# Moving the fourth weight strip's split behind the further blocks of an expert, and side-by-side high and low parts for short second and third blocks

## The chip, the cores and the metric

The kernel runs on one core of a Trainium2 chip. The metric is the time of one execution on the device in microseconds (us); of several runs the median counts.

## The reference

One decoder layer on 2048 tokens of 1024 channels, all in fp32. A first half (projections, a state-space branch, a convolution branch, gates, an output projection, a LayerNorm) gives `h`. The second half, which matters here, is a mixture of 32 SwiGLU experts of inner width 256. Every token picks two experts, so there are 4096 assignments:

```
hid = silu(xb @ w_gate[e]) * (xb @ w_up[e])      # xb: rows of h that chose expert e
y   = hid @ w_down[e]                            # added to the token's row with its weight
out = LayerNorm(ALPHA * h + sum of the two y)
```

The reference, run on its own inputs, sends these numbers of rows to experts 0 to 31:

```
121  75 114  74 129  25 158 106 205 200 227  36 276 286 255 177
 50  58 174 160  11 119 273  99  42  54 130 211  60  77  19  95
```

In blocks of 128 rows that is 49 blocks. Seventeen of them are a second or third block of their expert. Nine of those hold at most 64 rows: the second blocks of experts 4, 6, 15, 18, 19 and 26 (1, 30, 49, 46, 32 and 2 rows) and the third blocks of 12, 13 and 22 (20, 30 and 17 rows).

## The kernel before, in words

The program is one list of instructions for each engine, in an order written by hand; an instruction waits only where its data or its buffer is not ready. fp32 precision comes from splitting every operand into a high part (fp32r) and a low part, and from three matmuls for each product: high by high, high by low, low by high.

**Routing.** In the output projection, for each pair of token tiles, `route1` picks the experts, `rank` (on PE) numbers the rows within an expert and `route2` (lines 1189 to 1210) turns the number into a slot of a table `td` in DRAM and scatters token and weight there, four POOL DMAs a pair. The last pair's `route2` runs after the last output projection. Then ACT reads the table back (`lists`, line 1380), POOL gathers the rows of expert 0 from `hd`, and PE starts on the experts.

**The expert loop** (lines 1520 to 1552) goes over e = 0 to 31, with two sets of buffers, j = e % 2. Weights come in six strips for each expert: strips 0 to 3 are gate and up weights (128x1024 each, in `eraw`, split into `egu`), strips 4 and 5 are the down weights (`erd`, split into `edn`). `high` (line 1242) is ACT's copy to the high part, `low` (line 1247) DVE's subtraction that leaves the low part; `step` does both. While expert e is computed, the strips of expert e+1 are split, and the weights of e+3 are loaded by SP into the buffer that the split has emptied: `load` in four DMAs of 512 KB, the first two for strips 0 and 1, the last two for strips 2 and 3, and `load2` with one of 1 MB.

One round for expert e, in program order:

1. POOL gathers the rows of the block after (e+1, 0) and, if e has more than 128 (256) rows, those of the block after (e, 1) (and after (e, 2)).
2. `step` of strips 0, 1, 2 of e+1, then `high` of strip 3.
3. `block` (line 1471): `gateup`, 24 matmuls `pg<-egu,bhl` (eight channel strips times three products) into one PSUM bank, then `act`: ACT's Silu of the gate half, DVE's product with the up half (`hid`).
4. `low` of strip 3, and the four `load` DMAs of e+3.
5. `turn`: PE turns the rows of the next block (8 transposes `pt`), ACT copies the high part and DVE subtracts for the low part of `bhl`.
6. `down` of the expert before (12 matmuls `pd`).
7. `further(e, 1)` (line 1476), a branch at line 1486 that PE, ACT, DVE and POOL each take for themselves. With more than 128 rows it turns `hid` (two transposes `ph`), emits the finished rows (ACT copies PSUM to `yy` in two halves; between them `splith`, which is `hh` on ACT and `hl` on DVE; then POOL's scatter with addition into `acc`), and does block, turn and down for the second block, and inside it the same for a third. With fewer rows it only turns `hid`.
8. The end-of-expert `emit` with `splith`, then `high` and `low` of strips 4 and 5 of e+1, and `load2` of e+3.

`bhl` is a tile of 128 partitions, 8 strips, 2 parts (high, low) and 128 columns (rows of the block). `gateup` takes one part of one strip, 128x128, as the stationary operand and 512 columns of weights as the moving one.

`select` (line 1383) works out on DVE, from the table and the counts, which rows are gathered after which block (`NX`) and which rows and weights each emit uses (`LL`, `LQ`).

Of the kernel before, what the change touches and what calls it, by code (L numbers as in the profile page):

```python
# [10 lines left out]
F32 = mybir.dt.float32  # L11
# [15 lines left out]
NE = 32  # L27
# [58 lines left out]
def layer(ctx, tc, a, out, dbg=None):  # L86
# [976 lines left out]
    def small(name, shape, dt=F32):  # L1063
        return dp.tile([128] + list(shape), dt, name=name, bufs=2)
# [124 lines left out]
    def route2(p, pk):  # L1189
        ef, oh, ob, sd = RT_.pop(p)  # L1190
        for t in range(2):
            V.tensor_tensor(ohs, ohs, ob[:, t, :], op=OP.add)
        V.tensor_tensor(oh, oh, pk.unsqueeze(2).to_broadcast([128, 2, 2, 32]), op=OP.mult)

        rk, sl = small("r_rk", [2, 2]), rc_.tile([128, 2, 2], I32, name="r_sl", bufs=2)
        V.tensor_reduce(rk, oh, axis=AX.X, op=OP.add)
        dv = oh[:, :, :, 0]
        V.tensor_scalar(dv, rk, 1.0 / 128.0, -0.498, op0=OP.mult, op1=OP.add)
        V.scalar_tensor_tensor(rk, rk, 32.0, ef, op0=OP.mult, op1=OP.add)
        V.tensor_scalar(dv, dv, MAGIC, None, op0=OP.add)  # L1200
        V.tensor_scalar(dv, dv, MAGIC, -65535.0, op0=OP.subtract, op1=OP.mult)
        V.scalar_tensor_tensor(sl, rk, 16.0, dv, op0=OP.mult, op1=OP.add)
        for t in range(2):
            for k in range(2):
                G.memset(spacer, 0.0)
                d = G.indirect_dma_start(out=td, out_offset=bass.IndirectOffsetOnAxis(ap=sl[:, t, k:k + 1], axis=0),  # L1206
                                         in_=sd[:, t, k, :], in_offset=None)
                for o in SC:
                    tc.declare_no_dep(d.ins, o.ins, reason="other rows of the table")
                SC.append(d)  # L1210
# [146 lines left out]
    HH = ep.tile([128, 2, 128], F32R, name="hh")  # L1357
    HL = ep.tile([128, 2, 128], F32R, name="hl")
    HID = ep.tile([128, FF], F32, name="hid")
    TAB = ep.tile([128, NE, JB, 2], I32, name="tab")  # L1360
    MK = ep.tile([128, NE, JB], F32, name="mk")
    OH = ep.tile([128, NE, JB], F32, name="ohb")
# [14 lines left out]
    V.tensor_tensor(OH[:, :, 0:JB - 1], MK[:, :, 0:JB - 1], MK[:, :, 1:JB], op=OP.subtract)  # L1377
    V.tensor_copy(OH[:, :, JB - 1:JB], MK[:, :, JB - 1:JB])

    def lists(e, n):  # L1380
        A.dma_start(TAB[:, e:e + n].rearrange("p e b c -> p e (b c)"), dap(td, 32 * e, [[1024, 128], [32, n], [1, 2 * JB]]))

    def select():


        V.tensor_copy(TF[:, 0:NE], TAB[:, :, :, 0])
        V.memset(TF[:, NE:NE + 1], float(1 << 20))
        first = TF[:, 1:NE + 1, 0:1]
        t = LP[:, :, 0:JB - 1, 0]
        V.tensor_tensor(t, TF[:, 0:NE, 1:JB], first.to_broadcast([128, NE, JB - 1]), op=OP.subtract)  # L1390
        V.tensor_tensor(t, t, MK[:, :, 1:JB], op=OP.mult)
        V.tensor_tensor(NX[:, :, 0:JB - 1], t, first.to_broadcast([128, NE, JB - 1]), op=OP.add)
        V.tensor_copy(NX[:, :, JB - 1:JB], first)
        V.tensor_tensor(LP[:, :, :, 0], TF[:, 0:NE], OH, op=OP.mult)
        V.tensor_tensor(LP[:, :, :, 1], TAB[:, :, :, 1].bitcast(F32), OH, op=OP.mult)
        lf = TF[:, 0:NE, 0:2]
        V.tensor_reduce(lf, LP.rearrange("p e b c -> p e c b"), axis=AX.X, op=OP.add)
        V.tensor_copy(LL[:, :, 0], lf[:, :, 0])
        V.tensor_copy(LL[:, :, 1].bitcast(F32), lf[:, :, 1])
        V.tensor_copy(LP[:, :, 0:JB - 1, 0], TAB[:, :, 0:JB - 1, 0])  # L1400
        V.tensor_tensor(LP[:, :, 0:JB - 1, 0], LP[:, :, 0:JB - 1, 0], OH[:, :, 1:JB], op=OP.mult)
        V.tensor_tensor(LP[:, :, 0:JB - 1, 1], TAB[:, :, 0:JB - 1, 1].bitcast(F32), OH[:, :, 1:JB], op=OP.mult)
        V.tensor_tensor(LP[:, 1:NE, JB - 1], lf[:, 0:NE - 1], OH[:, 1:NE, 0:1].to_broadcast([128, NE - 1, 2]), op=OP.mult)
        V.memset(LP[:, 0:1, JB - 1], 0.0)
        V.tensor_reduce(lf, LP.rearrange("p e b c -> p e c b"), axis=AX.X, op=OP.add)
        V.tensor_copy(LQ[:, :, 0], lf[:, :, 0])
        V.tensor_copy(LQ[:, :, 1].bitcast(F32), lf[:, :, 1])
# [30 lines left out]
    def act(i):  # L1438
        A.activation(HID, PG[i][:, 0:FF], AF.Silu)
        V.tensor_tensor(HID, HID, PG[i][:, FF:2 * FF], op=OP.mult)  # L1440

    def turnh():
        for k in range(2):
            PE.transpose(PH[:, k, :], HID[:, 128 * k:128 * k + 128], ident)

# [24 lines left out]

    def block(e, b, i, gu):

        gateup(i, gu)
        act(i)

    def further(e, b):

# [29 lines left out]
    load2(2, 0)  # L1507
    lists(0, 2)
    lists(2, NE - 2)
    gather(X1, TAB[:, 0, 0, 0:1])  # L1510
    high(1, 2, 3, 4, 5)
    low(1, *range(6))
# [7 lines left out]
    for e in range(NE):  # L1520
# [10 lines left out]
                    gather(X2, NX[:, e, 2:3])  # L1531
        if more:
            step(1 - j, 0, 1, 2)
            high(1 - j, 3)
        block(e, 0, j, GU[j])
        if more:
            low(1 - j, 3)
            if e + 3 < NE:
                load(e + 3, 1 - j)
        turn(XN[j])  # L1540
        if e:
            down(1 - j)
        further(e, 1)
        if e:
            emit(LQ[:, e, 0:1], LQ[:, e, 1:2], splith)
        else:
            splith()
# [167 lines left out]
```

## Time and profile before

| | |
|---|---|
| median of 3 runs | 1854.08 us (1853.65 to 1859.51) |
| the profiled execution | 1854.43 us, its span 1852.7 us |
| PE, PEld, DVE busy | 92%, 74%, 71% of the span |
| ACT, POOL busy | 37%, 17% |
| the expert stage, first to last gate-and-up block | 1281.3 to 1771.9 us of the span |
| mean granted TensorE clock | 0.968 |

PE is TensorE's matmuls, PEld its loads of stationary operands, which overlap them; DVE is VectorE, ACT ScalarE, POOL GpSimd, SP the queue that issues most loads. Busy shares are means over stages with different limits, so the stretches below are read one by one. A matmul's row lasts longer than its distance to the next (they are pipelined), so PE's pace is read from the starts. In a timeline a square bracket gives the engine's idle time before the row and what ended it; DVEq L1486 is DVE's own passing of the branch of `further`. Line 66 is the helper through which all PE and DVE instructions go.

### The profile page before, as it was taken

The page shows a single profiled execution, that of the slowest core. Times are in us where ns is not written, and L with a number is a line of the kernel's source. Part 1 is how long each engine was busy: PE and PEld are TensorE (multiplying, and loading weights), DVE is VectorE, ACT ScalarE, POOL GpSimd, SP SyncE. Part 2 cuts the span into 40 slices and gives each one's busy share as a digit, 9 for nine tenths or more (in the row PEclk, how much of TensorE's full clock was granted, in tenths as well). Part 3 has the DMA queues.
Part 4 walks back from the last instruction along what each step waited for, and adds up shares of the span by engine and source line. Part 5 has one row for each costly group of instructions (what it writes and reads, how often), then busy time and mean ns, then how long its engine had stood idle before and what let it go on. Part 6 is the DMA issues. An engine that isn't in the chain of part 4 may idle for free. (4 is left out here: it accounts for less than half of the span.)

```text
span 1852.7 us, 23925 instructions
## 1 busy us (share of the span) xinstructions
PE 1703.9 (92%) x8368; PEld 1371.0 (74%) x8369; DVE 1317.4 (71%) x2429; ACT 692.4 (37%) x1069; POOL 312.6 (17%) x319
## 2 busy tenths in 40 slices
PE   8999999999999999999999999973999999999930
PEld 7888877777777778777888888862777787777730
DVE  5798787777876874766576778885675556657648
ACT  5111221222222222633321122324675556666744
POOL 2000001101110101000000012212343233333315
PEclk9999999999999999999999999986999999999975
DMA  6321432432342336333463423546988878789755
GB/s 215 95 92 46 119 78 71 145 98 77 100 149 70 101 99 222 109 122 114 172 191 119 148 92 115 182 164 197 304 266 256 253 211 253 230 261 327 223 176 231
DMA packets 214027, 300.81 MB, mean 162 GB/s; under 512 B 29391, under 2 KB 159521, under 8 KB 211313
## 3 DMA queue, kind: packets, MB, share of 16 engines
q1 hardware_dynamic: 166496, 213.32, 35.0%
q0 software_dynamic: 23152, 56.06, 11.6%
q10 hardware_dynamic: 24224, 29.47, 4.8%
q8 instruction: 86, 1.41, 0.3%
q14 instruction: 69, 0.56, 0.1%
HBM read 224.77 MB, written 92.31 MB: 171 GB/s over the span
## 5 line engine op out<-in xcount | busy, mean ns | idle before, releaser
L66 PE MATMUL mm<-xh,whi 128*128 128x512 f32 x896 | 360.8, 403 | 0.0
L66 PE MATMUL mm<-xl,whi 128*128 128x512 f32 x896 | 353.6, 395 | 0.0
L66 PE MATMUL mm<-xh,wlo 128*128 128x512 f32 x896 | 352.1, 393 | 0.0
L66 PE MATMUL pg<-egu,bhl 128*128 128x512 f32 x1176 | 287.4, 399 | 25.1 <-DVEq L1486 20.7
L66 DVE SCALAR_TENSOR_TENSOR cvw<-cvw,cw 128x1024 f32<-128x1024 f32 x240 | 292.1, 1280 | 0.0
L66 PEld LDWEIGHTS pg<-egu,bhl 128*128 128x128 f32 x1176 | 217.9, 189 | 78.1 <-issue 14.2
L66 PEld LDWEIGHTS mm<-xh,whi 128*128 128x128 f32 x896 | 168.3, 188 | 47.9 <-ACT y L712 5.8
L66 PEld LDWEIGHTS mm<-xh,wlo 128*128 128x128 f32 x896 | 168.2, 188 | 41.6
L66 PEld LDWEIGHTS mm<-xl,whi 128*128 128x128 f32 x896 | 168.6, 188 | 36.5 <-DVE xl L66 0.3
L66 PE MATMUL mm<-yt,whi 128*128 128x512 f32 x512 | 163.7, 401 | 2.0 <-ACT yt L858 1.5
L66 PE MATMUL mm<-wo,mh 128*128 128x512 f32 x512 | 162.5, 398 | 0.0
L66 DVE TENSOR_TENSOR egu<-eraw,egu 128x1024 fp32r<-128x1024 f32 x128 | 150.7, 1218 | 6.0 <-ACT egu L1245 5.9
L731 ACT ACTIVATE gt<-mm,cols 128x512 f32<-128x512 f32 x64 | 44.0, 688 | 265.4 <-PE mm L66 254.4
L66 PE MATMUL pd<-edn,hh 128*128 128x512 f32 x392 | 126.7, 404 | 1.0 <-ACT hh L1447 1.0
L1245 ACT ACTIVATE egu<-eraw 128x1024 fp32r<-128x1024 f32 x128 | 124.9, 1056 | 3.3 <-DMA td<-r_sd,r_sl 3.1
L66 PEld LDWEIGHTS mm<-yt,whi 128*128 128x128 f32 x512 | 96.6, 190 | 25.8 <-ACT yt L858 1.5
L66 PEld LDWEIGHTS mm<-wo,mh 128*128 128x128 f32 x512 | 94.2, 188 | 21.5 <-issue 1.2
L66 PE MATMUL mm<-yt,wlo 128*128 128x512 f32 x256 | 101.5, 396 | 0.0
L66 PE MATMUL mm<-wo,ml 128*128 128x512 f32 x256 | 101.0, 394 | 0.0
L66 DVE TENSOR_TENSOR edn<-erd,edn 128x1024 fp32r<-128x1024 f32 x64 | 75.7, 1225 | 33.0 <-ACT edn L1245 33.0
L1206 POOL DMA_INDIRECT td<-r_sd,r_sl x32 | 38.2, 1194 | 310.3 <-DVE r_sl L66 300.9
L1465 POOL DMA_INDIRECT acc<-yy,lq x31 | 49.2, 1589 | 244.8 <-ACT yy L1462 244.8
(300 smaller groups left out, 2561.3 us busy)
## 6 DMA issues: line engine op xcount, KB each, us to landing
eraw<-in_w_gate_dram SPq DMA_DIRECT2D x64, 512.0 KB
eraw<-in_w_up_dram SPq DMA_DIRECT2D x64, 512.0 KB
erd<-in_w_down_dram SPq DMA_DIRECT2D x32, 1024.0 KB
gd<-gt ACTq DMA_DIRECT2D x64, 256.0 KB
gl<-gd SPq DMA_DIRECT2D x64, 256.0 KB
wraw<-in_w_in_dram SPq DMA_DIRECT2D x28, 512.0 KB
xt<-in_x_dram SPq DMA_DIRECT2D x16, 512.0 KB
rg<-in_x_dram SPq DMA_DIRECT2D x8, 1024.0 KB
```

What stands on the lines that cost most here:

```text
L66: return f(*args, **kw)
L731: A.activation(gt, p, AF.Sigmoid, bias=cols[:, BI + 12 + m:BI + 13 + m])
L1206: d = G.indirect_dma_start(out=td, out_offset=bass.IndirectOffsetOnAxis(ap=sl[:, t, k:k + 1], axis=0), in_=sd[:, t, k, :], in_offset=None)
L1245: A.activation(h, src, AF.Copy)
L1465: G.indirect_dma_start(out=acc, out_offset=bass.IndirectOffsetOnAxis(ap=idx, axis=0), in_=y, in_offset=None, bounds_check=S - 1, oob_is_er ...
```

## The change

Four things are done.

- **Slots.** `route2` numbers the rows of a block so that the first 64 go to the even partitions (0, 2, 4, ...) and the next 64 to the odd ones. That takes eight small DVE operations in place of five.
- **Short blocks.** A second or third block of at most 64 rows goes through `gateup_small` and `act_small`. Its stationary operand is every second column of both parts of a strip, 64 high columns and 64 low ones side by side (`BE`), against the high and then the low part of the weights: 16 matmuls in place of 24. PSUM rows 0 to 63 then hold the products of the high parts, rows 64 to 127 those of the low parts; ACT copies the lower half to SBUF, DVE adds the upper one, and Silu and product follow on 64 rows. The choice is a branch inside the branch of `further`, on the same four engines. First blocks are untouched.
- **Lists.** A second copy of the table, `TB2`, read by one more DMA on ACT's queue, holds the rows of even slots close together; `select` gets eight more DVE operations and the set-up before it eight (`SM`, `NM`: which experts end in a short block), so that the emit of a short block writes the right rows. ACT zeroes `HID` once.
- **The fourth strip.** `high` of strip 3 leaves its place ahead of the first block, `low` of strip 3 and the `load` of e+3 leave theirs behind it. All three stand after `further(e, 1)` and before the end-of-expert emit.

```
 route2:
         dv = oh[:, :, :, 0:2]
         V.tensor_scalar(dv[:, :, :, 0], rk, 1.0 / 128.0, -0.498, op0=OP.mult, op1=OP.add)
+        V.tensor_scalar(dv[:, :, :, 1], rk, 1.0 / 64.0, -0.498, op0=OP.mult, op1=OP.add)
-        V.scalar_tensor_tensor(rk, rk, 32.0, ef, op0=OP.mult, op1=OP.add)
+        V.scalar_tensor_tensor(rk, rk, 64.0, ef, op0=OP.mult, op1=OP.add)
         V.tensor_scalar(dv, dv, MAGIC, None, op0=OP.add)
-        V.tensor_scalar(dv, dv, MAGIC, -65535.0, op0=OP.subtract, op1=OP.mult)
-        V.scalar_tensor_tensor(sl, rk, 16.0, dv, op0=OP.mult, op1=OP.add)
+        V.tensor_scalar(dv, dv, MAGIC, None, op0=OP.subtract)
+        V.tensor_scalar(dv[:, :, :, 0], dv[:, :, :, 0], -1023.0, None, op0=OP.mult)
+        V.scalar_tensor_tensor(dv[:, :, :, 0], dv[:, :, :, 1], -65024.0, dv[:, :, :, 0], op0=OP.mult, op1=OP.add)
+        V.scalar_tensor_tensor(sl, rk, 16.0, dv[:, :, :, 0], op0=OP.mult, op1=OP.add)
 ...
+    T = ep.tile([64, 512], F32, name="tt")
+    BE = B.rearrange("p k q (r t) -> p k (q r) t", t=2)[:, :, :, 0]
 ...
+    A.activation(HID, zero[:, 0:FF], AF.Copy, scale=0.0)
 ...
+    def gateup_small(i, gu):
+        p = PG[i]
+        for k in range(8):
+            t = gu[k // 4]
+            for q in range(2):
+                PE.matmul(p, BE[:, k], t[:, q, k % 4, :], start=k == 0 and q == 0, stop=k == 7 and q == 1)
+
+    def act_small(i):
+        A.activation(T, PG[i][64:128], AF.Copy)
+        V.tensor_tensor(T, T, PG[i][0:64], op=OP.add)
+        A.activation(HID[0:64], T[:, 0:FF], AF.Silu)
+        V.tensor_tensor(HID[0:64], HID[0:64], T[:, FF:2 * FF], op=OP.mult)
 ...
     def block(e, b, i, gu):
-        gateup(i, gu)
-        act(i)
+        if not b:
+            gateup(i, gu)
+            act(i)
+            return
+        with tc.If(CNT[e] > 128 * b + 64) as c:
+            gateup(i, gu)
+            act(i)
+        with c.Else():
+            gateup_small(i, gu)
+            act_small(i)
 ...
     lists(2, NE - 2)
+    A.dma_start(TB2.rearrange("p e b c -> p e (b c)"), dap(td, 0, [[2048, 64], [32, NE], [1, 2 * JB]]))
     gather(X1, TAB[:, 0, 0, 0:1])
 ...
         if more:
             step(1 - j, 0, 1, 2)
-            high(1 - j, 3)
         block(e, 0, j, GU[j])
-        if more:
-            low(1 - j, 3)
-            if e + 3 < NE:
-                load(e + 3, 1 - j)
         turn(XN[j])
         if e:
             down(1 - j)
         further(e, 1)
+        if more:
+            step(1 - j, 3)
+            if e + 3 < NE:
+                load(e + 3, 1 - j)
         if e:
             emit(LQ[:, e, 0:1], LQ[:, e, 1:2], splith)
```

## Rows read from the trace of the kernel before

**Rows 1.** Busy time by stretch, all engines: start and end, us, then PE, PEld, DVE, ACT and POOL busy with their instructions, granted clock, DMA share and GB/s. The stretches are from the last routing to the first expert's rows, the experts, and the last LayerNorm.

```profile
1255.00:1281.00 26.00, 1.49 (x7) 1.52 (x8) 14.01 (x39) 11.39 (x13) 7.69 (x10) 0.50 0.88 261
1281.00:1790.00 509.00, 471.44 (x2257) 380.97 (x2255) 306.92 (x378) 319.09 (x479) 167.65 (x96) 0.99 0.80 240
1790.00:1853.00 63.00, 0.00 (x0) 0.00 (x0) 53.59 (x104) 27.41 (x52) 25.96 (x16) 0.50 0.68 267
```

**Rows 2.** Who waited for whom in the expert stage (1270 to 1790 us): engine, tile and line, what it waited for, us in total, times, longest.

```profile
PE pg L66 <- DVEq L1486: 20.7, 15, 2.0
...
ACT yy L1462 <- DMA acc<-yy,ll: 17.1, 6, 3.1
...
PE pg L66 <- DVE bhl L66: 4.2, 6, 0.8
```

**Rows 3.** Timeline of PE in the expert stage: start, us, engine, line, operation, count and idle time before. The gate-and-up blocks are those of expert 0 (the first of 49), 3, 4 (its first and its second block), 5, 6 and 31 (the last); the `ph` row ends expert 3, the `pt` row is the turn in expert 4's second block.

```profile
1281.29 6.49 PE L66 MATMUL pg<-egu,bhl 128*128 128x512 f32 x24
...
1311.14 5.75 PE L66 MATMUL pg<-egu,bhl 128*128 128x512 f32 x24 [1.72 <-DVEq L1486]
...
1320.40 0.38 PE L66 MATMUL ph<-ident,hid 128*128 128x128 f32 x2
1321.69 5.79 PE L66 MATMUL pg<-egu,bhl 128*128 128x512 f32 x24 [0.91 <-DVEq L1486]
...
1331.08 5.79 PE L66 MATMUL pg<-egu,bhl 128*128 128x512 f32 x24
1336.71 1.04 PE L66 MATMUL pt<-ident,xhi 128*128 128x128 f32 x8
...
1340.52 5.76 PE L66 MATMUL pg<-egu,bhl 128*128 128x512 f32 x24
...
1352.61 5.80 PE L66 MATMUL pg<-egu,bhl 128*128 128x512 f32 x24 [1.98 <-DVEq L1486]
...
1766.32 5.74 PE L66 MATMUL pg<-egu,bhl 128*128 128x512 f32 x24 [0.90 <-DVEq L1486]
```

**Rows 4.** Timeline of DVE from the end of expert 2 to that of expert 3, both of one block. The first and the last row are the two low parts of a `turn`, the single `egu` row is `low` of strip 3.

```profile
1309.66 1.28 DVE L66 TENSOR_TENSOR bhl<-pt,bhl 128x512 fp32r<-128x512 f32 x2
1311.53 0.42 DVE L66 TENSOR_TENSOR hl<-ph,hh 128x256 fp32r<-128x256 f32 x1 [0.59 <-ACT hh L1447]
1313.06 2.36 DVE L66 TENSOR_TENSOR edn<-erd,edn 128x1024 fp32r<-128x1024 f32 x2 [1.10 <-ACT edn L1245]
...
1319.07 1.22 DVE L66 TENSOR_TENSOR egu<-eraw,egu 128x1024 fp32r<-128x1024 f32 x1
1320.21 1.28 DVE L66 TENSOR_TENSOR bhl<-pt,bhl 128x512 fp32r<-128x512 f32 x2
```

**Rows 5.** Timeline of ACT over the same experts, and its first emit after expert 4's second block.

```profile
1311.11 0.38 ACT L1447 ACTIVATE hh<-ph 128x256 fp32r<-128x256 f32 x1 [1.02 <-DVEq L1486]
...
1317.91 1.09 ACT L1427 ACTIVATE bhl<-pt 128x512 fp32r<-128x512 f32 x2
1320.76 0.69 ACT L1462 ACTIVATE yy<-pd,lq 128x512 f32<-128x512 f32 x1 [1.75 <-PE ph L66]
...
1341.45 0.69 ACT L1462 ACTIVATE yy<-pd,lq 128x512 f32<-128x512 f32 x1 [2.96 <-DMA acc<-yy,ll]
```

**Rows 6.** POOL's gather of the rows that expert 4's second block turns, and the median times from issue to landing of such gathers and of the scatters that a second block issues (DMA issues of the whole run); last, SP's third load of that round (timeline).

```profile
1327.18 1.93 POOL L1413 DMA_INDIRECT xhi<-hd,nx  x1 [0.30 <-issue]
...
xhi<-hd,nx POOLq DMA_INDIRECT x30, 8.7
acc<-yy,ll POOLq DMA_INDIRECT x15, 8.8
...
1330.90 1.76 SPq L1223 DMA_DIRECT2D eraw<-in_w_gate_dram  x1
```

**Rows 7.** Groups of instructions in the expert stage, shapes apart: busy us, mean ns of one, idle before.

```profile
L66 PE MATMUL pg<-egu,bhl 128*128 128x512 f32 x1176 | 287.4, 399 | 25.1 <-DVEq L1486 20.7 <-DVE bhl L66 4.2
L66 PEld LDWEIGHTS pg<-egu,bhl 128*128 128x128 f32 x1176 | 217.9, 189 | 78.1 <-issue 14.2 <-ACT yy L1462 8.2 <-DVE bhl L66 8.2
...
L1245 ACT ACTIVATE egu<-eraw 128x1024 fp32r<-128x1024 f32 x120 | 117.0, 1057 | 0.2 <-issue 0.2
...
L66 DVE TENSOR_TENSOR bhl<-pt,bhl 128x512 fp32r<-128x512 f32 x100 | 64.3, 684 | 11.6 <-ACT bhl L1427 11.6
...
L1462 ACT ACTIVATE yy<-pd,lq 128x512 f32<-128x512 f32 x62 | 42.7, 688 | 55.4 <-PE ph L66 36.1 <-DMA acc<-yy,ll 17.1 <-PE pd L66 2.2
```

**Rows 8.** The branch of `further` on PE's sequencer: count, shortest, median and longest in ns.

```profile
L1486 PEldq COMPARE_BRANCH  x60: 65/179/1325, 1285.3 to 1772.1; - x60
```

**Rows 9.** Busy time by stretch (columns as in rows 1): expert 4 with its two blocks, and expert 17.

```profile
1321.00:1340.00 19.00, 18.31 (x89) 15.11 (x90) 11.39 (x15) 11.47 (x18) 7.22 (x4) 1.00 1.05 336
...
1561.00:1572.00 11.00, 10.60 (x43) 8.64 (x44) 9.14 (x11) 8.11 (x11) 3.68 (x2) 0.84 1.06 356
```

**Rows 10.** From routing to the first expert: two of the last `route2`'s DVE operations, ACT's issue of the two list reads, DVE's first use of the lists, PE's first turn.

```profile
1255.00 0.37 DVE L66 TENSOR_SCALAR r_oh<-r_oh 128x4 f32<-128x4 f32 x2
...
1264.26 0.93 ACTq L1381 DMA_DIRECT2D tab<-td  x2
...
1272.26 0.21 DVE L66 CAST tf<-tab 128x96 f32<-128x96 int32 x1 [1.30 <-DMA tab<-td]
...
1279.52 1.94 PE L66 MATMUL pt<-ident,xhi 128*128 128x128 f32 x8 [25.09 <-DMA xhi<-hd,tab]
```

More of the change, by code (lines that the diff above doesn't have):

```diff
@@ L1196, in route2 @@
         V.tensor_reduce(rk, oh, axis=AX.X, op=OP.add)
-        dv = oh[:, :, :, 0]
-        V.tensor_scalar(dv, rk, 1.0 / 128.0, -0.498, op0=OP.mult, op1=OP.add)
-        V.scalar_tensor_tensor(rk, rk, 32.0, ef, op0=OP.mult, op1=OP.add)
+        dv = oh[:, :, :, 0:2]
+        V.tensor_scalar(dv[:, :, :, 0], rk, 1.0 / 128.0, -0.498, op0=OP.mult, op1=OP.add)
+        V.tensor_scalar(dv[:, :, :, 1], rk, 1.0 / 64.0, -0.498, op0=OP.mult, op1=OP.add)
+        V.scalar_tensor_tensor(rk, rk, 64.0, ef, op0=OP.mult, op1=OP.add)
         V.tensor_scalar(dv, dv, MAGIC, None, op0=OP.add)
-        V.tensor_scalar(dv, dv, MAGIC, -65535.0, op0=OP.subtract, op1=OP.mult)
-        V.scalar_tensor_tensor(sl, rk, 16.0, dv, op0=OP.mult, op1=OP.add)
+        V.tensor_scalar(dv, dv, MAGIC, None, op0=OP.subtract)
+        V.tensor_scalar(dv[:, :, :, 0], dv[:, :, :, 0], -1023.0, None, op0=OP.mult)
+        V.scalar_tensor_tensor(dv[:, :, :, 0], dv[:, :, :, 1], -65024.0, dv[:, :, :, 0], op0=OP.mult, op1=OP.add)
+        V.scalar_tensor_tensor(sl, rk, 16.0, dv[:, :, :, 0], op0=OP.mult, op1=OP.add)
         for t in range(2):
@@ L1359, in layer @@
     HID = ep.tile([128, FF], F32, name="hid")
+    T = ep.tile([64, 512], F32, name="tt")
+    BE = B.rearrange("p k q (r t) -> p k (q r) t", t=2)[:, :, :, 0]
+    TB2 = ep.tile([64, NE, JB, 2], I32, name="tab2")
+    SM = ep.tile([128, NE], F32, name="sm")
+    NM = ep.tile([128, NE], F32, name="nm")
+    TF2 = ep.tile([64, NE, 2], F32, name="tf2")
+    A.activation(HID, zero[:, 0:FF], AF.Copy, scale=0.0)
     TAB = ep.tile([128, NE, JB, 2], I32, name="tab")
@@ L1378, in layer @@
     V.tensor_copy(OH[:, :, JB - 1:JB], MK[:, :, JB - 1:JB])
+    V.memset(SM, 0.0)
+    for b in range(1, JB):
+        V.tensor_scalar(NM, pc, 128.0 * b + 64.0, None, op0=OP.is_le)
+        V.tensor_tensor(NM, NM, OH[:, :, b], op=OP.mult)
+        V.tensor_tensor(SM, SM, NM, op=OP.add)
+    V.tensor_scalar(NM, SM, -1.0, 1.0, op0=OP.mult, op1=OP.add)
     def lists(e, n):
@@ L1397, in select @@
         V.tensor_reduce(lf, LP.rearrange("p e b c -> p e c b"), axis=AX.X, op=OP.add)
+        V.tensor_tensor(lf, lf, NM.unsqueeze(2).to_broadcast([128, NE, 2]), op=OP.mult)
+        lp, l2 = LP[0:64], TF2
+        V.tensor_copy(lp[:, :, :, 0], TB2[:, :, :, 0])
+        V.tensor_tensor(lp[:, :, :, 0], lp[:, :, :, 0], OH[0:64], op=OP.mult)
+        V.tensor_tensor(lp[:, :, :, 1], TB2[:, :, :, 1].bitcast(F32), OH[0:64], op=OP.mult)
+        V.tensor_reduce(l2, lp.rearrange("p e b c -> p e c b"), axis=AX.X, op=OP.add)
+        V.tensor_tensor(l2, l2, SM[0:64].unsqueeze(2).to_broadcast([64, NE, 2]), op=OP.mult)
+        V.tensor_tensor(lf[0:64], lf[0:64], l2, op=OP.add)
+        V.scalar_tensor_tensor(lf[64:128, :, 0], SM[64:128], float(1 << 20), lf[64:128, :, 0], op0=OP.mult, op1=OP.add)
         V.tensor_copy(LL[:, :, 0], lf[:, :, 0])
```

## The prediction

> **What bounds the kernel now.** I read the busy times by stretch first. The whole change lies in two of them: 26 us between routing and experts, in which PE stands almost still, and 509 us of experts, in which PE is busy for 471 [rows 1]. What comes before and after keeps its time.
>
> Within the expert stage I went to PE's timeline. A block that nothing holds up takes 9.39 us from the start of its gate-and-up matmuls to the next (expert 4's first block, 1321.69 to 1331.08), and that is PE's own work. From the first to the last of the 49 blocks it is 485.03 us, or 48 steps of 10.10 [rows 3]. Against 48 x 9.40 = 451.2 that leaves 33.8 us in which PE is held up. The table of waits names most of it: 20.7 us in 15 waits for DVE to pass the branch of `further`, and 4.2 for the low parts of the turned rows [rows 2]. There are exactly fifteen one-block experts from 2 to 30. Another 1.8 us went to the clock: expert 17's 11 us have a mean granted clock of 0.84, so some 3.5 of them ran at 1.2 GHz [rows 9].
>
> The timelines of DVE and ACT say why DVE is late. In a one-block expert DVE goes from the end of one turn's low part (1310.94) to the end of the next (1321.49) in 10.55 us, the very step PE makes (1311.14 to 1321.69), and it rests for only 0.59 + 1.10 us of it, once for `hh` and once for `edn`. `low` of strip 3 stands directly ahead of the turn's low part, and takes 1.14 us from its start to the next [rows 3, 4]. So DVE is the bound in these fifteen, and strip 3 lies on its path although the next block needs it only at its 18th matmul.
>
> **The move of strip 3.** DVE's next low part ends 1.14 us earlier, and the pass itself falls behind the branch, where DVE rests for 1.69 us: 10.55 - 1.14 = 9.41. ACT's copy falls between the turn's copy and the emit, where ACT waits 1.75 us for `ph` [rows 5]; it takes 1.06 [rows 7], so it is hidden. What is late next is the emit: the first `yy` starts 0.36 us after `ph`, `hh` can start 0.58 later, and from `hh` to the end of the next low part it is 1311.11 to 1321.49, 10.38, less 1.14. That is 10.18 us after `ph`, while PE comes round in 9.4. Two one-block experts in a row then take 9.4 and 10.2 us, 9.8 in the mean: 0.75 saved each. Behind an expert with a further block (seven times) the chain begins late anyway: the step 1340.52 to 1352.61 took 12.09 us because the emit had waited for the second block's scatter until 1341.45 [rows 3, 5]. There strip 3 falls into that wait, and the full 1.14 is saved. Sum: 7 x 1.14 + 8 x 0.75 = 14.0 us.
>
> The other 33.8 - 20.7 = 13.1 us are lost in experts with further blocks and to the slow clock; the second block starts and stalls on the low part behind strip 3. Of that I take 8. Against it stands POOL: the rows that a second block turns are gathered after the emit, and by the median of 8.7 us the gather issued at 1327.18 lands at 1335.9, 0.8 us before the turn at 1336.71 [rows 3, 6]. As blocks start up to 1.1 us sooner after the emit, 14 experts meet a new wait of about 0.3, 4 us. Net of the move: 14 + 8 - 4 = 18 us. Bounds: 10 (half, where emit and gather hold the rest) and 28 (33.8 less 0.8 in each of seven).
>
> The loads move too. The half of `load` for strips 2 and 3 left SP at 1330.90 in expert 4 [rows 6] and will leave about 9 us later there, 2.4 later in a one-block expert. Its data are needed a whole expert later, and SP has only the 1 MB down load behind it, which waits for strip 5 either way. I cost it at nothing; what hides it is the spare time of that expert, and without it ACT's `high`, in order ahead of Silu, would wait. It also takes 1 MB out of the stretch in which the DMA share is 1.05 [rows 9], which may bring the second block's scatter home sooner.
>
> **The short blocks.** Matmuls follow each other every (5.79 - 0.40) / 23 = 0.234 us [rows 3, 7], so eight fewer save 1.87 us in each of nine blocks, 16.9 in all. The tail behind them grows: an ACT copy from PSUM of 512 columns (0.69, as `yy`), a DVE addition (0.68, as `bhl`) [rows 7], then Silu (256 columns, as `hh`: 0.38), the turn's two copies (1.09) [rows 5] and its last low half (0.68), 3.5 us in a row and about 3.8 with the hand-overs. PE has turn, `down` and `ph` to do meanwhile, 3.8 us in expert 4's second block (1336.71 to 1340.52 [rows 3]), so I charge 0.2. In the three third blocks the rows for the turn were gathered right behind those of the second, a block earlier than they are needed: 3 x 1.6 = 4.8 us. In the six second blocks the turn would come 1.87 us sooner but its rows land when they land: the 0.8 us of slack, less what the move has used. I take 0.5 each, 3 us. Together 7.8. No row has a stationary operand read at every second column. If its load took twice 189 ns [rows 7], 0.38 would set the pace, and 16 matmuls would take 6.0 us, 0.4 more than the 24. I take the same pace, for 189 leaves 45 ns spare; the ends are -4 (all nine slower) and +15 (the gather not in the way). The Trainium skill ("SBUF — State Buffer", section "Door 1: The DMA port swizzle") says that reads with at least two hits in a 16-byte line keep full bandwidth, four fp32 of stride for free; no run here shows it yet.
>
> **What is added elsewhere.** `route2` has three more small DVE operations, each some 0.19 us apart [rows 10]. Seven calls lie beside PE's matmuls; the last is on the way to the table: +0.6. `TB2` is 64 x 32 small pieces, about half of the 128 x 30 in the lists that landed 7.5 us after their issue (1264.7 to 1272.2), and it shares the DMA engines with the gather for which PE waits [rows 10]: +1.0, between 0 and 4. `select` starts at 1272.26, 7.3 us before PE's first turn; its operations, now 27 of about 0.2 us like the first, fit in; the eight of the set-up and ACT's zeroing lie in the 25 us wait for the table and the rows. The new branch costs PE's sequencer 0.18 us (median) and runs ahead of PE's queue [rows 8]; I charge 0.6 for all 17. Sum +2.2 us.
>
> **Sum.** -18.0 - 7.8 + 2.2 = -23.6. The profiled execution took 1854.43 us (1.7 of it around its span of 1852.7), 0.35 above the median: 1830.8, **1831 us**.
>
> **Rivals.**
> 1. *The rows come in time.* With 1 MB out of the way gathers and scatters land a microsecond or two sooner, the six second blocks keep 1.67 us in place of 0.5 (-7) and the 4 us of new waits for the gather are gone: 1831 - 7 - 4 = 1820. For it: DMA share 1.05 there. Against: the down load and the first half still precede the gather's rows. Chance 0.14.
> 2. *The emit holds the stage.* After further blocks ACT waits for the scatter (17.1 us [rows 2]); its landing does not move, short blocks save nothing and the move gives 10: 1854.4 - 10 + 2.2 = 1847. Chance 0.18.
> 3. *The branch becomes the bound* (slower). With 34 more loads and matmuls in each skipped body, PE's jumps reach code not at hand. The longest branch took 1325 ns, one of 60 [rows 8]. If each of 17 inner and 29 skipped outer branches (18 experts without a second block, 11 with a second and no third) cost that on PE's path, 61 us come to the sum: 1892. It decides from 0.64 us each (46 x 0.64 = 29.2, slower by 5.6). Against: the median is 179, and none of PE's listed waits is a branch of its own. The Trainium skill ("Runtime: NRT & Kernel Launch", section "Instruction fetch mechanics") states that a taken branch outside the window of instructions at hand waits for a fetch; by that rule more skips would miss. The 1325 ns row may be such a case, the other 59 are not. Chance 0.05.
> 4. *The later load comes too late* in the 14 experts with further blocks: slower by 6 only if each waits 2.2 us; 1862 then. Chance 0.03.
> 5. *The short path is not taken* or its matmuls are paced by the load of their operand: 1839 to 1843, just above the forecast's own range. Chance 0.05.
>
> **How the numbers follow.** Forecast as summed: chance 0.55, its own range 1823 to 1840. The range reaches to rival 1 with both terms at their bounds (1854.4 - 28 - 15 + 2.2 = 1814), and to rival 2: 1814 to 1847. About 0.3% (5.6 us) is what a measurement can tell from no change. Faster than that: 0.55 + 0.14 + 0.05 and 0.15 of rival 2's 0.18, 0.89. Within it: the 0.03 left of rival 2 and 0.02 of rivals 3 and 4 in a mild form, 0.05. Slower: the rest of rivals 3 and 4, 0.06.
>
> **What would show it.** Right: `low` of strip 3 after the branch and the 20.7 us of waits for DVE's branch below 10; steps behind one-block experts of 9.4 and 10.2; 1104 matmuls `pg` in place of 1176, at the same 0.234 us; a new wait of PE's `pt` for the gathered rows. Wrong: `pg` loads of 0.3 us or more; ACT's `egu` waiting for DMA; PE's `pg` waiting for its own branch; steps of one-block experts still at 10.5.

## The result and the profile after

The changed kernel takes 1841.09 us in the median (1836.82 to 1844.63), against 1856.01 for the kernel before, timed beside it: a ratio of 0.9917, 95% interval [0.9888, 0.9946], some 15 us faster. The forecast was 1831, its range 1814 to 1847. The profiled execution is the longest of the four, 1844.63 us with a span of 1843.0, so its rows show 9.7 us of gain, not 15.

Busy time by stretch of the changed kernel (columns as in [rows 1]):

```profile
1255.00:1281.00 26.00, 2.67 (x15) 2.25 (x16) 16.71 (x58) 14.74 (x18) 6.39 (x10) 0.50 0.83 238
1281.00:1780.00 499.00, 460.22 (x2182) 372.41 (x2181) 319.44 (x406) 328.12 (x487) 169.38 (x98) 0.97 0.82 250
1780.00:1843.00 63.00, 0.00 (x0) 0.00 (x0) 53.47 (x104) 27.42 (x52) 25.97 (x16) 0.50 0.67 267
```

PE has 11 us less to do in the expert stage, and from the first block's start to the last one's it takes 476.6 us in place of 485.0. The table of waits (columns as in [rows 2]) says what PE stood still for:

```profile
PE pg L66 <- ACT edn L1249: 6.3, 2, 3.5
PE pg L66 <- DVEq L1537: 5.9, 8, 1.1
POOL xhi L1442 <- DVE lp L66: 5.6, 1, 5.6
...
PE pg L66 <- DVE bhl L66: 3.8, 1, 3.8
PE pt L66 <- DMA xhi<-hd,nx: 3.6, 3, 1.8
```

The wait for DVE's branch went from 20.7 us to 5.9, as forecast [rows 2], and the turn's new wait for gathered rows is there (3.6). New, and not forecast, are 3.8 us in one wait for `bhl` and 6.3 in two waits put down to ACT's `edn`, which had long been done.

The short blocks, by form (columns as in [rows 7]):

```profile
L66 PE MATMUL pg<-egu,bhl 128*128 128x512 f32 x1104 | 274.9, 405 | 17.2 <-ACT edn L1249 6.3 <-DVEq L1537 5.9 <-DVE bhl L66 3.8
L66 PEld LDWEIGHTS pg<-egu,bhl 128*128 128x128 f32 x1104 | 210.1, 194 | 66.1 <-ACT edn L1249 6.7 <-DVE bhl L66 4.5 <-issue 3.8
```

There are 1104 matmuls in place of 1176, and a load takes 194 ns in place of 189. That is the mean over all 1104; the 144 loads of the short blocks alone, which read every second column, take 195 in the mean (sixteen loads of expert 26's second block: 3.0 us busy), and a block's other loads stand at 188 in the median. So reading every second column costs nothing on PE's path.

The start of the stage is one place where it goes wrong. First PE (columns as in [rows 3]), then DVE, then ACT, all of the changed kernel:

```profile
1278.86 1.94 PE L66 MATMUL pt<-ident,xhi 128*128 128x128 f32 x8 [20.92 <-DMA xhi<-hd,tab]
1280.63 1.22 PE L66 MATMUL pg<-egu,bhl 128*128 128x512 f32 x2
1285.60 7.05 PE L66 MATMUL pg<-egu,bhl 128*128 128x512 f32 x22 [3.75 <-DVE bhl L66]
...
1296.42 7.22 PE L66 MATMUL pg<-egu,bhl 128*128 128x512 f32 x24 [1.01 <-DVEq L1537]
...
1307.30 5.79 PE L66 MATMUL pg<-egu,bhl 128*128 128x512 f32 x24
```

```profile
1279.41 0.20 DVE L66 CAST tf<-tab 128x96 f32<-128x96 int32 x1
...
1284.86 1.28 DVE L66 TENSOR_TENSOR bhl<-pt,bhl 128x512 fp32r<-128x512 f32 x2
```

```profile
1269.62 0.94 ACTq L1400 DMA_DIRECT2D tab<-td  x2
1270.60 3.13 ACTq L1561 DMA_DIRECT2D tab<-td  x1
1273.78 2.00 ACT L1249 ACTIVATE egu<-eraw 128x1024 fp32r<-128x1024 f32 x2 [7.98 <-issue]
```

`select` begins at 1279.41, not at 1272.26 [rows 10]: behind PE's first turn, not 7.3 us ahead of it. From the first block's start to the third's it takes 26.67 us; it was 18.48.

Two things in these rows are not the new read's cost. The list reads themselves are issued 5.4 us later in this execution (1269.62 against 1264.26 [rows 10]), and 4.0 us of that already stand at `route2`'s last operation, which writes the slots: it starts at 1259.4, against 1255.4 before and 1255.4 to 1256.7 in the nine other kernels of this study that have the new `route2`, so that some 3 us belong to this execution alone. And the first block starts early: its turn comes 9.2 us behind the list reads, where it came 15.3 behind them before. A step from block start to block start counts that lead as a loss; experiment 5 takes it out.

Adding up the steps from block to block (the starts of the gate-and-up rows in PE's timelines) shows every part at once. All columns come from the profiled execution of that kernel; the last three are experiments told below (1, 4 and 10).

| us, from block start to next block start | before | changed | move alone | second table read later | mended start, gathers reordered |
|---|---|---|---|---|---|
| blocks 0 and 1 (start) | 18.48 | 26.67 | 19.71 | 19.73 | 19.45 |
| 15 one-block experts | 166.49 | 162.57 | 152.38 | 159.62 | 162.36 |
| 14 first blocks of experts with more | 132.63 | 133.49 | 133.00 | 134.05 | 136.02 |
| 8 further blocks over 64 rows | 79.41 | 77.68 | 76.96 | 76.31 | 75.41 |
| 6 short second blocks | 59.80 | 52.69 | 58.15 | 55.16 | 46.89 |
| 3 short third blocks | 28.25 | 23.52 | 28.24 | 23.48 | 23.54 |

### The profile page after: what moved, and what is told of

The parts are those of the page before. It is cut to its first block, busy times and chain, and to the rows that moved or that the text cites. A ratio compares the mean times of both kernels' runs of the same rounds, so it can differ in the third digit from the quotient of the medians.

```text
span 1843.0 us, 23964 instructions
## 1 busy us (share of the span) xinstructions
PE 1697.9 (92%) x8296; PEld 1365.3 (74%) x8297; DVE 1331.6 (72%) x2478; ACT 701.6 (38%) x1079; POOL 312.3 (17%) x319
## 3 DMA queue, kind: packets, MB, share of 16 engines
q0 software_dynamic: 23152, 56.06, 11.3%
## 4 chain that ended last, share of the span: by engine, by line
PE 64%; DMA 18%; issue 11%; DVE 5%; POOL 0%; POOLq 0%; ACT 0%; another core or an unknown queue 0%; SPq 0%; DVEq 0%; ACTq 0%
PE mm L66 51%; DMA acc<-yy,lq 10%; PE aux L66 7%; DMA acc<-yy,ll 4%; PE pg L66 4%; DMA td<-r_sd,r_sl 2%; PE pd L66 2%; DVE f L66 1%; DVE cvw L66 1%; DVE f_q L66 1%; PE pt L66 1%; DMA xhi<-hd,nx 1%; DMA gd<-gt 0%; DMA xt<-in_x_dram 0%; DMA cn<-nw 0%
## 5 line engine op out<-in xcount | busy, mean ns | idle before, releaser
L66 PE MATMUL pg<-egu,bhl 128*128 128x512 f32 x1104 | 274.9, 405 | 17.2 <-ACT edn L1249 6.3
L66 PEld LDWEIGHTS pg<-egu,bhl 128*128 128x128 f32 x1104 | 210.1, 194 | 66.1 <-ACT edn L1249 6.7
L66 DVE TENSOR_TENSOR egu<-eraw,egu 128x1024 fp32r<-128x1024 f32 x128 | 150.8, 1219 | 18.5 <-ACT egu L1249 16.1
```

Source lines behind the costliest of these rows:

```text
L66: return f(*args, **kw)
```

## The experiments

A ratio is to the kernel before, timed beside it on the same chip (its median was 1854 to 1859 us), with its 95% interval; kernels that were not timed beside each other are compared by ratio. Each interval is some 2 to 5 us to either side, so a difference of two ratios that is smaller than that tells nothing by itself.

**1. The move alone.** The kernel before with the last part of the change only:

```
 step(1 - j, 0, 1, 2)
-high(1 - j, 3)
 block(e, 0, j, GU[j])
-low(1 - j, 3)
-load(e + 3, 1 - j)
 turn(XN[j]); down(1 - j); further(e, 1)
+step(1 - j, 3)
+load(e + 3, 1 - j)
```

> The kernel before with the fourth strip's high, low and load moved behind the further blocks, and nothing else (old slots, no short path, no second table). Theory A (the move gives what was worked out, and the change lost its gain at the start of the expert stage and in PE's branches): no second table on ACT's queue, so the first two blocks start 9.1 and 9.4 us apart as before; the bodies that PE skips are as long as before, so at most one or two of its branches take over 0.6 us; 18 us faster than before, about 1837. Theory B (the emit and the gathered rows hold the one-block experts, the move is worth only half): 8 to 10 us, about 1846, steps of one-block experts above 10.3 us in the mean.

1836.75 us, ratio 0.9904 [0.9889, 0.9919]: 18.2 us by the medians. Theory A, but for the first two steps, which are 10.3 and 9.4 us, not 9.1 and 9.4. The longest of PE's branches is 0.85 us. Two one-block experts in a row (2 and 3) start at these times:

```profile
1300.29 5.81 PE L66 MATMUL pg<-egu,bhl 128*128 128x512 f32 x24
...
1310.56 5.75 PE L66 MATMUL pg<-egu,bhl 128*128 128x512 f32 x24 [0.61 <-DVEq L1486]
...
1320.21 2.10 PE L66 MATMUL pg<-egu,bhl 128*128 128x512 f32 x8
```

Steps of 10.27 and 9.65, near the 10.2 and 9.4 that the forecast had for the emit and PE as bounds in turn. PE's waits for DVE's branch come to 5.6 us, from 20.7 [rows 2]. Against this kernel the whole change is 3 us slower by the medians and 2.4 by the ratios (0.9917 and 0.9904), whose intervals overlap: all the rest of the change, short blocks included, gains nothing that can be told.

**2. Everything but the move.** The changed kernel with strip 3 and the load at their old place.

> The changed kernel with the fourth strip's high, low and load at their old place (slots, second table, lists and short path stay). Theory A: the start costs its 7 to 8 us, PE's branches some 5, short blocks give back 8 to 11 (they lose the stall on low parts only in part): 1852 to 1858, no faster than before. Theory B (short blocks carry the change, the move little): 1844 to 1848.

1857.2 us, ratio 1.0012 [1.0000, 1.0024]. Theory A: the short path, lists and slots by themselves gain nothing. Blocks 0 and 1 take 27.38 us, while short blocks give back 16.1 (59.80 + 28.25 to 48.52 + 23.44). Most of what they give is lost elsewhere in the stage: the first blocks of experts with more take 140.06 us in place of 132.63, where PE now stands ahead of the second block (8.7 us in five waits put down to ACT's `yy`), and the one-block experts 173.17 in place of 166.49.

**3. A mended start.** The changed kernel with three edits:

```
-A.activation(HID, zero[:, 0:FF], AF.Copy, scale=0.0)
-A.dma_start(TB2 ...)                  # ahead of
 high(1, 2, 3, 4, 5)
+A.dma_start(TB2 ...)                  # behind
 select()                              # now ends with NX
 gather(XN[0], NX[:, 0, 0:1])
 turn(X1)
+select2()                             # LL, LQ
```

> The changed kernel with three things altered at the start of the expert stage: the read of the second table is issued by ACT behind its eight copies of expert 1's strips in place of ahead of them; the part of select that makes the emit lists stands behind the first turn; HID is not zeroed. Theory A: DVE reaches the first turn's low part and POOL the second gather some 5 to 7 us sooner, block 0 to block 2 takes 18.5 to 19.5 us in place of 26.7, the kernel is about 7 us faster than the changed one: 1834. Theory B (the late start is the table scatter's own lateness, or a chance of that execution): within 2 us of the changed kernel, 1839 to 1843.

1832.2 us, ratio 0.9879 [0.9863, 0.9896]. Theory A: blocks 0 and 1 take 19.80 us (it said 18.5 to 19.5), and the kernel is 7 us faster than the changed one by ratio (9 by the medians; the intervals just touch).

**4. Of these, the one line.** Only the read of the second table moved behind ACT's copies (four, not eight as the expectation says).

> The changed kernel with one line moved: ACT issues the read of the second table behind its eight copies of expert 1's strips in place of ahead of them. The mended start was worth 9 us in three edits. Theory A (the 3.13 us that ACT spends on that issue, in front of everything DVE and POOL wait for, is the larger part): 5 to 7 us faster than the changed kernel, 1834 to 1836, blocks 0 to 2 in 20 to 22 us. Theory C (the zeroing of HID, which puts the table load of Silu behind the first block, and the emit lists ahead of the first turn are the larger part): 2 us or less, 1839 to 1841.

1834.94 us, ratio 0.9880 [0.9859, 0.9902]: Theory A, at the upper end of its 5 to 7 us: by ratio one line gives what the three edits gave (either gain over the changed kernel is known to some 6 us either way). PE's start in this kernel, and ACT:

```profile
1280.41 6.47 PE L66 MATMUL pg<-egu,bhl 128*128 128x512 f32 x24
...
1290.65 5.83 PE L66 MATMUL pg<-egu,bhl 128*128 128x512 f32 x24 [1.00 <-DVEq L1537]
...
1300.14 1.18 PE L66 MATMUL pg<-egu,bhl 128*128 128x512 f32 x4
```

```profile
1266.54 2.79 ACTq L1563 DMA_DIRECT2D tab<-td  x1
1267.33 1.04 ACT L1249 ACTIVATE egu<-eraw 128x1024 fp32r<-128x1024 f32 x1
```

The first block is no longer interrupted, though `select` is as long as in the changed kernel (5.5 us). ACT's issue still takes 2.79 us, but the copies, now ahead of it in ACT's program, run beside it.

**5. The issue without its use.** The move alone, plus the read of a second table at the change's place, that nothing waits for.

> The kernel with the moved fourth strip alone, and the read of a second table issued by ACT where the change has it, ahead of its four copies of expert 1's strips 2 to 5 (an earlier expectation counted eight); nothing uses what is read, so nobody waits for it to land. Theory A (what costs at the start is the time that ACT is held by the issue, in front of DVE's low parts, select and the second gather): blocks 0 to 2 take 25 to 28 us in place of 19.7, 5 to 8 us slower than the move alone: ratio to the kernel before 0.993 to 0.995. Theory C (it was the wait for the second table's data, or the longer select): blocks 0 to 2 in 19.5 to 21 us, ratio 0.990 to 0.991.

1837.45 us, ratio 0.9894 [0.9875, 0.9914]. Neither theory's numbers: blocks 0 and 1 take 22.96 us, 3.2 more than with the move alone, and the time shows no loss that this comparison can tell. ACT:

```profile
1268.00 4.76 ACTq L1511 DMA_DIRECT2D tab<-td  x1
1272.81 2.00 ACT L1245 ACTIVATE egu<-eraw 128x1024 fp32r<-128x1024 f32 x2 [8.13 <-issue]
```

By the steps the issue alone would be about half of the 7 us that lie between 26.67 and 19.71. The time does not show it, and the rows say why. What counts is when the third block starts, and the steps begin at the first block, whose own start moves. Counted from the issue of the list reads:

| us behind the list reads | first block starts | third block starts |
|---|---|---|
| before | 17.0 | 35.5 |
| move alone | 16.9 | 36.7 |
| changed | 11.0 | 37.7 |
| experiment 2 (everything but the move) | 11.0 | 38.3 |
| experiment 3 (mended start) | 12.6 | 32.4 |
| experiment 4 (the one line) | 15.0 | 34.8 |
| this one | 12.7 | 35.7 |

In the three kernels here whose ACT is held ahead of its copies (changed, experiment 2, this one) the first gathered rows reach PE 4.3 to 4.5 us after POOL's issue, against 8.4 to 8.6 before, with the move alone and in experiment 4. SP's next loads go out later there too: they wait for DVE's low parts of the strips that ACT copies (the first at 1276.3 here, 9.3 us behind the list reads; at 1268.1 and 4.5 behind them with the move alone). That the gather lands sooner because of this is likely, and not tested. So, in one execution of each, the issue alone delays the third block by nothing (35.7 against 36.7), and in the changed kernel the place of that one line is worth 2.9 us (37.7 against 34.8). There the rest of the change stands behind a late ACT: `select` lasts 5.45 us (1279.41 to 1284.86) in place of 3.48 (1278.45 to 1281.93 here), and zeroing `HID` puts the load of Silu's table (1.28 us) behind the first block's matmuls; it starts at 1292.73 in the changed kernel, at 1282.11 in the kernel before.

**6. A body that is longer and no cheaper.** The move alone, with two equal arms:

```
+with tc.If(CNT[e] > 128 * b + 64) as c:
     gateup(i, gu); act(i)
+with c.Else():
+    gateup(i, gu); act(i)
```

> The kernel with the moved fourth strip alone, with a second and third block's gate-and-up in two arms of a branch that are both the full 24 matmuls with Silu and product (no slots, no second table, no short path): more code in the bodies that are skipped, no less work. Theory A (long branches of PE come with longer skipped bodies): four or more branches or gaps of PE over 1 us, 6 to 10 us slower than with the move alone: 1843 to 1847. Theory B (they come with the second table, the short path or chance): 0 to 2 us slower, 1837 to 1839, at most one long branch.

1863.26 us, ratio 1.0030 [1.0016, 1.0044]: over 20 us slower than the move alone, more than twice what theory A said. The fifteen one-block experts take 175.4 us in place of 152.4. In the middle of one of them:

```profile
1667.72 2.00 PE L66 MATMUL pg<-egu,bhl 128*128 128x512 f32 x8
1675.98 0.57 PE L66 MATMUL ph<-ident,hid 128*128 128x128 f32 x2 [2.58 <-issue]
1677.15 8.42 PE L66 MATMUL pg<-egu,bhl 128*128 128x512 f32 x24 [0.60 <-ACT yy L1462]
```

At 1669.8 PE's sequencer took 6.0 us for the branch of `further`, so `ph` was late. Six more of these branches took 1.0 to 6.2 us, and three times the sequencer stood 2.5 to 3.4 us where neither a long branch nor a wait is on record.

**7. Shorter bodies.** The version of experiment 10 (below) with the short path in second blocks only: third blocks take 24 matmuls again.

> The mended start with the gathers in the other order (0.985 of the kernel before), with the short path in second blocks only; third blocks always take 24 matmuls. The body that PE skips in a one-block expert is 32 loads and matmuls shorter. The three third blocks give 4.8 us back. Theory A (PE's long branches come with the length of the skipped body): two or three of the six long branches or gaps stay, the fifteen one-block experts take 155 us in place of 162, 1 to 4 us faster than with both short paths: ratio 0.983 to 0.9845. Theory B (it is the second branch level itself, not its length): as many long branches, 5 us slower: 0.987.

1834.74 us, ratio 0.9898 [0.9882, 0.9913], outside both forecasts. Of the branches theory A is right, and more so than it said: none takes over 0.88 us, though two gaps ahead of the inner branch are 1.3 and 1.4; one-block experts fall from 162.36 to 157.14 us, third blocks pay 4.7. The stage from first to last block is 1 us shorter; its first block starts 4.2 us later (1283.62). The list reads are issued only 0.7 us later than in experiment 10; the gather of the first rows is issued 1.7 us later, and its rows reach PE 9.8 us after that in place of 7.4. Why is not settled.

The branch of `further` on PE's sequencer (count, shortest, median and longest in ns) in the move alone, the kernel of experiment 7, the changed kernel and experiment 6:

```profile
L1486 PEldq COMPARE_BRANCH  x60: 65/183/845, 1285.8 to 1754.8; - x60
```

```profile
L1539 PEldq COMPARE_BRANCH  x60: 65/196/875, 1287.9 to 1752.2; - x60
```

```profile
L1537 PEldq COMPARE_BRANCH  x60: 65/179/4387, 1290.2 to 1763.1; - x60
```

```profile
L1494 PEldq COMPARE_BRANCH  x60: 65/196/6213, 1285.1 to 1778.2; - x60
```

A one-block expert skips 96, 112, 128 and 144 matmuls with their loads in these four. The median does not move; the longest does. Over all kernels whose third block stands inside the second: with 96 or 112 skipped matmuls PE's longest branch is 0.68 to 1.34 us (five kernels; 1.33 in the kernel before [rows 8]), with 128 or 144 it is 3.1 to 6.3 us (seven). The long ones are not spread by chance: in the changed kernel and experiments 2, 3, 4 and 10 expert 29 has one each time, experts 7 and 20 in four of the five.

**8. Two jumps in place of one.** The third block's branch beside the second's, first with the last `ph` behind both, then (on the mended start) with a `ph` in each arm. The first, in short:

```
 with tc.If(CNT[e] > 128): turnh; emit; block; turn; down
 with tc.If(CNT[e] > 256): turnh; emit; block; turn; down
 turnh
```

> The changed kernel with the third block's branch beside the second's in place of inside it (for experts 1 to 31), and the last turn of hid behind both: a one-block expert jumps twice over one body in place of once over two. Theory A (PE's long branches, five of 1.5 to 4.4 us and a gap of 2.7 us at one in the changed kernel's profile, are waits for code behind a jump that is now too long): branches of PE over 1 us vanish or are rare, steps of one-block experts come to 9.5 to 10.3 us throughout, 6 to 10 us faster than the changed kernel: 1831 to 1835. Theory B (the long branches have to do with the amount of code or with busy DMA engines, not with the length of the jump): as many long branches, same time within 2 us, or 1 to 3 us slower for the added branches.

1862.2 us, ratio 1.0045 [1.0030, 1.0060]: over 20 us slower than the changed kernel, outside both forecasts. The longest branch is down to 1.99 us, as theory A says, and the time says that this was not the way to get there:

```profile
PEld ph L66 <- DVEq L1531: 20.4, 19, 2.8
...
PE pg L66 <- ACT hh L1490: 14.7, 19, 1.1
```

What stands behind the joined branch waits here for the other engines to pass it (DVEq L1531), and `ph` now stood there.

> The changed kernel with the mended start, and the third block's branch beside the second's; the transposes of hid stay inside the arms, one in each, so that PE need not wait for another engine's branch before them (it did, 20.4 us in 19 waits, in the version that was 21 us slower). Theory A: long branches of PE go (one or none over 1 us), and no new wait takes their place: 7 to 9 us faster than the mended start alone, 1823 to 1825. Theory B (the second branch of each one-block expert makes PE wait for the other engines to pass it): 1832 to 1842, with PE's gate-and-up matmuls waiting for DVE or ACT at that branch in the one-block experts.

1860.33 us, ratio 1.0010 [1.0000, 1.0020]; the mended start alone had 0.9879. PE waits as in theory B, but for `hh` and `hl`, and the time is 18 us above the 1842 at which that theory's range ended:

```profile
PE pg L66 <- ACT hh L1492: 18.2, 12, 3.8
PE pg L66 <- DVE hl L66: 18.2, 8, 4.3
```

And three branches still took 4.3 to 4.5 us, though each jump passes only half the code. The length of the jump alone does not explain the long branches.

**9. Branches that PE need not take.** The branches around the gathers on POOL alone, through a count that only POOL reads: on experiment 7, and on experiment 10.

> As the one with the short path in second blocks only, and the branches around the gathers of a round are taken by POOL alone (the count is read for POOL in a value of its own); PE, ACT and DVE pass no branch there. Theory A (PE stands at those two branches between the transposes of hid and the first gate-and-up matmul of the next expert, with the longest waits for code among them): long branches fewer still, the steps of one-block experts 0.2 to 0.5 us shorter, 3 to 6 us faster than with the branches on all engines: ratio 0.980 to 0.982. Theory B (PE waits for DVE and ACT there anyway, the waits for code only move to another instruction): same within 2 us.

> The mended start with the gathers in the other order and both short paths, with the branches around the gathers on POOL alone. Theory A (long waits for code come with the skipped length and hit these branches): 3 to 8 us faster than with the branches on all engines, ratio 0.980 to 0.983. Theory B (the wait for code comes wherever the jump ends): same time, the gaps stand ahead of another of PE's instructions: 0.984 to 0.986.

1835.57 us, ratio 0.9896 [0.9880, 0.9913], and 1831.68, ratio 0.9873 [0.9857, 0.9889]. No gain in either. The first is theory B (0.9898 without the edit). The second is above theory B's own 0.984 to 0.986, with an interval that overlaps experiment 10's (0.9847). With both short paths PE's longest branch is 6.34 us, at the branch of `further`, where the five long ones of experiment 10 (3.1 to 5.6 us) stand too.

**10. The gathers in the other order,** on the mended start:

```
+gather(X1, NX[:, e, 1:2])             # if e has over 128 rows; X2 as well
 gather(XN[1 - j], NX[:, e + 1, 0:1])
-gather(X1, NX[:, e, 1:2])
```

> The changed kernel with the mended start, and POOL's gathers of a round in the other order: first the rows that the second and third block's turns need in this expert, then those that the next expert's turn needs. Theory A (the short second blocks are held by their gathered rows): the gather for a second block is issued about 2 us sooner, the steps of the short second blocks of experts 4, 18 and 26 come from 9.2 to 9.8 us down to 7.9 to 8.3, 3 to 5 us faster than the mended start alone: 1827 to 1829. Theory B (they are held by DVE, ACT and the emit): 1831 to 1833.

1830.62 us, ratio 0.9847 [0.9829, 0.9866], the fastest version here, ahead of both kernels; by ratio 6 us faster than the mended start (theory A said 3 to 5), by the medians 1.6, and 2.3 in the stage of the profiled execution. Theory A: the second blocks of 4, 18 and 26 take 7.74, 8.02 and 8.03 us, and the six short ones 46.89 in place of 51.19. Of the turn in expert 26, in the changed kernel and in this one:

```profile
1697.62 3.96 PE L66 MATMUL pg<-egu,bhl 128*128 128x512 f32 x16
1703.60 1.06 PE L66 MATMUL pt<-ident,xhi 128*128 128x128 f32 x8 [2.01 <-issue]
```

```profile
1684.94 3.97 PE L66 MATMUL pg<-egu,bhl 128*128 128x512 f32 x16
1688.75 1.04 PE L66 MATMUL pt<-ident,xhi 128*128 128x128 f32 x8
```

## Why the prediction was right and wrong

Direction and range held; the forecast itself was 10 us too low. By its own steps:

- **The move: 18.0 forecast, 18.2 measured.** The one-block experts give 14.1 (166.49 to 152.38) where 14.0 stood, through the two mechanisms named: DVE no longer late, the emit next. The steps of 9.4 and 10.2 are there. That the sum fits so closely is partly luck: the seven behind further blocks give 6.9 where 8.0 stood, the eight others 7.2 where 6.0 stood. In the experts with more blocks it is 3.7 net of the worse places where 4 stood (132.63 + 79.41 + 59.80 + 28.25 = 300.09 against 296.35). That the loads move at nothing is part of this number.
- **Short third blocks: 4.8 forecast, 4.7 measured. Short second blocks: 3 forecast,** 3.0 in experiment 4 and 5.5 in the changed kernel's profile against the move alone. The reason given, gathered rows that land when they land, is shown: with the gather in front it becomes 11.3. The matmul pace was right too, (3.96 - 0.39) / 15 = 0.238 us, and the rule of the Trainium skill ("SBUF — State Buffer", section "Door 1: The DMA port swizzle") that a stride of up to four fp32 costs no bandwidth, agrees with the 195 ns of the short blocks' loads at stride 2.
- **The second table: 1.0 forecast (0 to 4), 3 measured** from the list reads (37.7 against 34.8, one execution of each), 7 by the steps (26.67 against 19.71 and 19.73), which count the first block's early start as well. The size is inside its bounds by the first count; the mechanism failed. Its price was taken from its size and landing, on the DMA side; what stands behind its issue on ACT, four copies that DVE's low parts, `select`, the second gather and the first turn's low part all wait for in a row, was not followed. The 3.13 us of the issue were in no row of before: the two list reads took 0.93 together [rows 10]. With that the next step fell too: `select` "fits in 7.3 us before PE's first turn" only as long as it starts there. And ACT's zeroing, costed at nothing, moved a load of Silu's table (1.28 us) behind the first block: after the first block's 6.47 us the next starts 3.77 us later in experiment 4, and 2.59 later where the zeroing is gone (7.81 of 10.40).
- **The inner branch: 0.6 forecast, at least 5 measured.** The one-block experts lose 10.2 of the 14.1 again (162.57), 7.2 in experiment 4. Not all of that is the branches: in experiment 7, which has no long one, they take 157.1, 5.2 less than in experiment 10, from which it differs by the third blocks' short path alone, and 4.8 more than with the move alone. This step failed too. The charge was a few hundredths of a us for each of 17, because the median branch takes 0.18 us [rows 8] and PE's queue hides it. The median still is 0.18; the cost is in the few long ones. Rival 3 had the mechanism with a chance of 0.05 and a price of 61 us, the longest row of before on every branch. In truth five branches of PE took 1.5 to 4.4 us and one stood 2.7 us ahead of its branch. Four of the five are at the branch of `further`, which PE's sequencer passes while its matmuls are still queued, so most of each is hidden: in expert 29 one took 4.39 us from 1742.3, PE's matmuls ran on until 1745.9, and the step is 10.77 us against 9.42 with the move alone. Not so behind the last `ph`, where nothing is queued. There stands the branch around POOL's gathers (line 1579), which the forecast did not price; PE has no matmul inside it. In expert 24 of the changed kernel:

```profile
L1579 PEldq COMPARE_BRANCH  x1: 3442/3442/3442, 1672.2 to 1672.2; - x1
```

```profile
1672.67 0.38 PE L66 MATMUL ph<-ident,hid 128*128 128x128 f32 x2
1675.86 8.54 PE L66 MATMUL pg<-egu,bhl 128*128 128x512 f32 x24 [2.80 <-ACT edn L1249]
```

  The wait is put down to `edn`; it is PE's own branch, for 3.44 us from 1672.2, a sign that the forecast had listed as proof against itself. Behind that pause the granted clock is 0.51 for 6 us, the level of 1.2 GHz, and the next block takes 8.54 us in place of 5.8:

```profile
1676.00:1682.00 6.00, 6.00 (x15) 4.67 (x16) 5.31 (x5) 3.29 (x4) 2.54 (x2) 0.51 1.10 318
```

- **What PE waits for in such a branch** no row shows. That the longest branch grows from 0.85 to 6.2 us as the skipped body grows from 96 to 144 matmuls, and that the kernel of experiment 6, with no other change than twin arms, loses over 20 us, shows the added code as the cause. The Trainium skill ("Runtime: NRT & Kernel Launch", section "Instruction fetch mechanics") says that a taken branch out of the window at hand waits for a fetch; the growth agrees with it; the 4.54 us with two half jumps and the 3.44 us at a branch with no matmul of PE inside do not follow from the length of one jump. Why some jumps of the same length pass in 0.2 us stays open; that the long ones come back at the same experts points to the place in the code.
- **Together,** from the sums of the table, changed less before: start +8.2, one-block experts -3.9, first blocks of the others +0.9, further blocks -1.7, short second -7.1, short third -4.7, in all -8.4 in the stage of the profiled execution; the start's +8.2 holds the first block's early start. With the start mended (experiments 3 and 4) the kernel is 22 us faster than before, near the 23.6 of the sum: the move and the third blocks gave what was said, the second blocks as much or more, and the branches took more.
- **Slips that change nothing:** the next block needs strip 3 at its 19th matmul, not the 18th, and two more arms of 16 put 32 loads and matmuls into the skipped body, not 34.

## What to carry to other kernels

An added DMA had two prices here, its transfer and the time that its queue's engine was held by the issue; follow what stands in that engine's program behind it, link by link, above all at a start where nothing covers it. Count a start from a fixed event ahead of it, not from a first block whose own start can move. A branch is not priced by its median: count the instructions that its bodies add on the busiest engine, look at the longest branch of the profile and not only the typical one, and try the longer body with no other change. Of several gathers on one queue, the one needed first goes first.

## What the runs showed of the hardware that was not expected

- Issuing a read of 64 x 32 pieces of 24 bytes took ACT's queue 2.79, 3.13 and 4.76 us in three kernels (2.5 to 4.8 in eleven), behind another read of 128 x 30 such pieces; the two reads ahead of it took 0.94 together.
- A COMPARE_BRANCH of PE, 0.18 us in the median, took up to 6.3 us; on DVE, ACT and POOL the sum over all their branches is 3.5 to 8.8 us in every kernel of this study, none over 0.07.
- Work behind a joined branch waited for DVE's passing of it: 20.4 us in 19 waits for two transposes put there.
